# Latent stages of an RWKV-7 hybrid: TensorE's order written out, head products moved into the chain's gaps

## Chip, cores and metric

One core of one Trainium2 chip runs the whole kernel. The metric is the device time of one execution in microseconds (us); the median of several runs is compared. The profiler records one execution, every instruction on the five engines: TensorE (PE, with its weight loads as PEld), VectorE (DVE), ScalarE (ACT), GpSimd (POOL) and SyncE (SP), the last two used here mostly to issue DMAs.

## What is computed

Two layers over 512 latent tokens and 256 context tokens of width 1024. The first ("even") layer is where the change lies. Its time mixing has 16 heads of 64, and per head and direction (forward and backward) a state S of 64 x 64 that is carried over the tokens:

```python
def step(S, inp):
    r_t, w_t, k_t, v_t, kk_t, a_t = inp
    sa = jnp.einsum("bhvk,bhk->bhv", S, -kk_t)
    S = (S * w_t[:, :, None, :]
         + sa[..., None] * (kk_t * a_t)[:, :, None, :]
         + v_t[..., None] * k_t[:, :, None, :])
    return S, jnp.einsum("bhvk,bhk->bhv", S, r_t)
```

The context tokens run first, and their final states start the scan over the latent tokens. The decay w and the factor a come from low-rank products (tanh and sigmoid of two thin matrices). In parallel runs a gated short convolution: four projections per 128 channels (cg, xb, bg, zb), a product, a three-tap filter and gates. An output projection joins both. The second ("odd") layer is a gated convolution module, which the change does not touch.

## The kernel before

The scan is done in chunks of 64 tokens, so the 512 latent tokens are 8 chunks (NLAT) and a chain has 8 steps. Heads are handled in pairs. There are twelve stages, `for s in range(12)` (L898): stages 0 to 3 run the context chains (two head pairs each), stages 4 to 11 the chains of latent pairs 0 to 7. While the chain of stage s runs, the same stage prepares later pairs. `STAGE` (L35) holds the order in which this is written for latent stages, "OSPLHFC":

- O, `po`: the bonus term of pair s+1, one product.
- S, `solve` (L629): the triangular inverse of each chunk of pair s+1. VectorE transposes Nt to X (L637), then does 31 pairs of dependent instructions, a product (L643) and an addition (L645); this text calls them the sweep. Two transposes follow (L648, here R1, and L649, R2). Then ScalarE copies R1 into E (L654), TensorE does the first merge (64 matmul records, 32 x 32), ScalarE copies Gs, TensorE does the second merge, ScalarE copies the result into E.
- P and L, `prep_lat` (L390) and `light` (`light0` L422, `lightz` L493): loads k, v, r of pair s+2 and makes its low-rank factors, normalised kk, and the operands AR and BK, one half for each direction z.
- H, `heavy` (L568): the head products of pair s+2. "A" makes four groups of 8 matmuls, A.B per chunk, which VectorE masks into E (L588); "N" copies diagonal blocks into Nt (L605, four copies on ScalarE); "B" transposes BK into BKt; "V" makes the centred v into UV.
- F, `finish` (L780): normalises the output O of pair s, transposes it and applies gate and bonus.
- C, `conv_branch` (L810): the dense projections of one 128-channel group of the convolution, 4 x 8 x 3 matmuls of 128 x 512. Three per product, since hi and lo parts are kept apart: `mm3` multiplies hi by hi, hi by lo and lo by hi. A weight half tile is loaded by DMA, cast to its hi part on ScalarE (L125), and subtracted to its lo part on VectorE (L126).

`chain_lat` (L723) is one chain step. It has three places where TensorE waits for another engine: after the products into zo, ScalarE copies Zs (L743); after the products into uh, ScalarE makes two UV copies (L749); after the products with BKt, VectorE updates H (L756, two instructions).

The order on each engine comes from a planner that simulates the program and takes, of the instructions that are ready on an engine, the one that was written first. What is written earlier thus goes first on ScalarE and VectorE too. Two means bend this: `pinned()` (L548) ties each matmul of a group to the one before, so that they keep the written order among themselves; the whole chain uses one such object, `cmm`. And `issue_after` puts a block behind a given instruction: `LIGHT_AFTER`, `HEAVY_AFTER` and `CONV_AFTER` name the chain steps behind which low-rank, head and dense products may start. Between those, the planner alone mixes dense and head products into the chain's gaps.

PSUM has eight banks of 128 x 512: two under the tag "at" (head and low-rank products), one each under mm0 and mm1 (projections), two under zo (chain), and uh0 and uh1. Weight half tiles have two buffers for the raw load and three each for hi and lo. Operands AR have six buffers, BK two, E and UV two each.

Of the kernel before, what the change touches and what calls it, by code (L numbers as in the profile page):

```python
# [8 lines left out]
F32 = mybir.dt.float32  # L9
# [20 lines left out]
LIGHT_AFTER = ((0, None, 0), (None, 1, 4))  # L30
HEAVY_AFTER = ((3, None, 3, 2), (5, None, None, None))
CONV_AFTER = (0, 2, 7, 6)
PA_ORDER = ((0, 1), (1, 0), (1, 1), (0, 0))
HEAVY = ("VBOAN", "ANBV")
STAGE = ("OFPLSH", "OSPLHFC")  # L35
# [16 lines left out]
def kernel(ctx: ExitStack, tc: tile.TileContext, I: dict, out: bass.AP):  # L52
# [6 lines left out]
    def mm3(o, ah, al, bh, bl, start, stop):  # L59
        T.matmul(o, ah, bh, start=start, stop=False)  # L60
        T.matmul(o, ah, bl, start=False, stop=False)  # L61
        T.matmul(o, al, bh, start=False, stop=stop)  # L62
# [52 lines left out]
    env = {"lo": V}  # L115
# [13 lines left out]
    def outproj(m0, tags, ks, held, early=lambda k: (None, None, None)):  # L129
        acc = [[bank(f"o{m0 + m}{n}", tags[2 * m + n]) for n in range(2)] for m in range(2)]  # L130
        for k in ks:
            y, yr, ws = early(k)
            if y is None:
                y = op.tile([P, 512], F32R, tag="y", name=f"y{m0}_{k}", bufs=4)
            yh, yl = y[:, 0:256], y[:, 256:512]
            if (m0, k) == (0, 7):
                hilo(oT7[:, 0:256], None, yh, yl, None)
            else:
                if yr is None:
                    yr = op.tile([P, 256], F32, tag="yr", name=f"yr{m0}_{k}", bufs=4)  # L140
                hilo(ysp[k, :, m0 * P : m0 * P + 2 * P], yr, yh, yl)
            if k not in held:
                if ws is None:
                    ws = [op.tile([P, D], F32, tag="wr", name=f"wr{m0}_{k}", bufs=3)] + [
                        op.tile([P, D], F32R, tag="w", name=f"w{x}{m0}_{k}", bufs=6) for x in "hl"]
                held[k] = hilo(wo[k * P : (k + 1) * P, :], *ws)
# [243 lines left out]
    def prep_lat(p):  # L390
        st = state(True, p)
        st["H"] = w("h0", f"h0_{p}")[:, 0:P].rearrange("p (z x) -> p z x", z=2)
        for which in (1, 2, 0):
            t = w("rkv"[which] + "_", "rkv"[which] + st["nm"])
            nc.gpsimd.dma_start(t, psp[p, which])
            st["rkv"[which]] = t
        nc.gpsimd.dma_start(st["H"], h0d[p].rearrange("p (z x) -> p z x", z=2))
        return st

# [14 lines left out]
    def light(st, an=None):  # L414
        la = LIGHT_AFTER[an is not None and an["lat"]]
# [6 lines left out]
    def light0(st):  # L422
# [23 lines left out]
        def low_(i, z, name):  # L446
            pl = ps_at(name)
            if lat:
                rows = slice(64 * i, 64 * i + 64)
                mm(pl, lwh[:, i, z, :], lorl[i][z], True, False)  # L450
                mm(pl, lwl[rows, z, :], lorl[i][z][rows], False, True)
# [10 lines left out]
        mm(pl, blk, sq, True, True)  # L462
# [105 lines left out]
    def heavy(st, an=None):  # L568
        ha = (None,) * 4 if an is None else HEAVY_AFTER[an["lat"]]
        lat, nm = st["lat"], st["nm"]  # L570
        v_ = st["v"]
# [4 lines left out]
        def pa():  # L576
            for gi, (z, g) in enumerate(PA_ORDER if lat else ((0, 0), (1, 0))):
                with anchored(an, ha[gi if lat else 2 * gi]):
                    AR, BK = st["AR"][z], st["BK"][z]
                    m, x = (4, P) if lat else (8, CH)  # L580
                    c0 = m * g
                    pas = [ch3(ps_at(f"pa{nm}{z}{g}{h}"), x) for h in range(2)]
                    go = pinned()
                    for c in range(m):
                        for h in (1, 0):
                            go(pas[h][:, c, :], kb(BK, h, c0 + c), AR[ZR[h], c0 + c, 0:x])
                    for h in range(2):
                        V.tensor_tensor(out=E[:, h, z * NLAT + c0 : z * NLAT + c0 + m, :], in0=pas[h],  # L588
                                        in1=maskE[:, z * (1 + h) : z * (1 + h) + 1, 0:x].to_broadcast([P, m, x]), op=ALU.mult)

        def pb():
            for z in range(2):
                pbs = [ch3(ps_at(f"pb{nm}{z}{h}")) for h in range(2)]
                go = pinned()
                for c in range(NLAT):
                    for h in (1, 0):
                        go(pbs[h][:, c, :], kb(st["BK"][z], h, c), ident[ZR[h], ZR[h]], op=tr)
                for h in range(2):
                    S.copy(st["BKt"][z][:, :, ZR[h]], pbs[h])
# [7 lines left out]
        def pv():  # L607
            pv = ch3(ps_at(f"pv{nm}"))
            for c in range(NLAT):
                for h in range(2):  # L610
                    mm(pv[ZR[h], c, :], v_[ZR[h], c * CH : (c + 1) * CH], ctr[ZR[h], ZR[h]], True, True)
# [6 lines left out]
        def po():  # L618
            if lat:
                bon = st["bon"]  # L620
                pb = ps_at("pbon" + nm)
                mm(pb, blk, bon, True, True)
                V.scalar_tensor_tensor(out=bon, in0=pb, scalar=0.5, in1=v_, op0=ALU.mult, op1=ALU.mult)

        st["po"] = po
        for x in HEAVY[lat]:
            {"A": pa, "B": pb, "N": nt, "V": pv, "O": po}[x]()

    def solve(st):  # L629
        nm, E = st["nm"], st["E"]  # L630
        Xt = w("X", "X" + nm)
# [18 lines left out]
        Gs = Xt[:, 0:512].rearrange("p (a b) -> p a b", b=32)  # L650
# [4 lines left out]
        pg = px = uhs[1]  # L655
        top = [slice(64 * z, 64 * z + 32) for z in range(2)]
        low = [slice(64 * z + 32, 64 * z + 64) for z in range(2)]
        for q in range(16):
            for z in range(2):
                mm(pg[low[z], q * 32 : q * 32 + 32], E[top[z], 1 - z, q, 32:64], R2[top[z], q, :],  # L660
                   True, True)
        for z in range(2):
            S.copy(Gs[low[z]], ch3(pg[low[z]], 32))
        for q in range(16):
            for z in range(2):
                mm(px[top[z], q * 32 : q * 32 + 32], Gs[low[z], q, :], R1[low[z], q, :], True, True)
# [56 lines left out]
    def chain_lat(st, i):  # L723
# [19 lines left out]
        S.copy(Zs, zo[:, 0:2, :])  # L743
        for h, z in hz:
# [3 lines left out]
        for h in range(2):  # L748
            u_ = S.copy(UV[ZR[1 - h], i : 2 * nch - i : 2 * nch - 1 - 2 * i, ZR[h]], uh[ZR[1 - h], 0:2, :])  # L749
        h_ = None  # L750
# [16 lines left out]
        else:  # L767
            o = O[:, nch - 1 - i : i + 1 : 2 * i + 1 - nch, :]
            V.tensor_tensor(out=o, in0=zo[:, 2:4, :], in1=o, op=ALU.add)

    def gate(p, cb, nm):
# [3 lines left out]
        g = cvp.tile([P, SEQ], F32, tag="gz", name=f"g{nm}{p}")  # L775
        S.activation(g, pz, AF.Tanh, scale=0.5)
        V.scalar_tensor_tensor(out=g, in0=g, scalar=1.0, in1=pz, op0=ALU.add, op1=ALU.mult)
        return g

    def finish(st):  # L780
# [10 lines left out]
        go = pinned()  # L791
# [15 lines left out]
    def after(anchor):  # L807
        return tc.issue_after(anchor) if anchor is not None else nullcontext()

    def conv_branch(p, an=None):  # L810
        anchors = [None if an is None or x is None else an[x] for x in ((0, 2, 4, 6) if p == 7 else CONV_AFTER)]
        with after(anchors[0]):
            wt = load_w(40 + p, f"cg{p}")
            pcg = ps_mm(f"pcg{p}")
            proj(wt, pcg, hlat)
        cg = cvp.tile([P, SEQ], F32, tag="cg", name=f"cg{p}")
        S.copy(cg, pcg)
        with after(anchors[1]):
            wt = load_w(48 + p, f"xb{p}")
            pxb = ps_mm(f"pxb{p}")  # L820
            proj(wt, pxb, hlat)
        V.tensor_tensor(out=cx[:, :, 1:65], in0=ch3(pxb), in1=ch3(cg), op=ALU.mult)
        yb = cvp.tile([P, SEQ], F32, tag="yb", name=f"yb{p}")
# [448 lines left out]
```

## Time and profile before

| what | us |
|---|---|
| median of 3 runs | 1514.84 (1505.89 to 1517.57) |
| profiled execution, its own time | 1506.4 |
| its span (first to last instruction) | 1504.6 |
| PE busy, DVE busy, ACT busy | 1429.3, 964.3, 766.4 |
| latent chains, first Zs copy to last stage's end | 541.5 to 1004 |
| second layer, after 1105 | 399 |

A row of a timeline reads: start, duration, engine, line of the kernel, operation, output<-inputs, shape, count; in brackets the idle time of that engine before it and what ended it. A row of a table of groups reads: line, engine, operation, tiles, shape, count | busy us, mean ns of one | idle us before, and what ended it. A row of a table by window reads: window, its length, then for each engine busy us and the number of instructions, the granted TensorE clock (1 is full), the share of time in which the DMA engines were busy, GB/s. An fp32 matmul leaves two records, so a group of 4 shows as x8. Tile names ending in l belong to latent pairs, in c to context pairs. Helpers hide the caller's line: L57 is every fp32 matmul, L60 to L62 the three dense ones of `mm3`.

### The profile page before, as it was taken

How to read it: one execution, taken by the hardware profiler on the slowest of the kernel's cores; microseconds unless marked ns; L12 is line 12 of the kernel's file. 1: busy time of each engine (PE TensorE's matmuls, PEld its weight loads, DVE VectorE, ACT ScalarE, POOL GpSimd, SP SyncE). 2: the span in 40 equal slices, each digit the busy share in tenths (PEclk: the TensorE clock that was granted, in tenths of full speed). 3: DMA queues.
4: the chain of work that ended last, by engine and by line, in shares of the span. 5: the costliest groups of instructions: out<-in, count | busy, mean ns of one | idle time of the engine just before them, and what ended most of it. 6: DMA issues, size and time to landing. Idle time of an engine off the chain costs nothing.

```text
span 1504.6 us, 29614 instructions
## 1 busy us (share of the span) xinstructions
PE 1429.3 (95%) x11857; PEld 1014.2 (67%) x11857; DVE 964.3 (64%) x2242; ACT 766.4 (51%) x1552; POOL 152.3 (10%) x263
## 2 busy tenths in 40 slices
PE   5699999999998999999999999999999999999998
PEld 1374577878776766666666666677757666688876
DVE  2575587558696978888788887658544525434333
ACT  4323465364755575755757657546553414363322
POOL 0533210000110101011011000001100000000000
PEclk9899999979997999999999999999999999999999
DMA  8644533212232312231222212468403303033222
GB/s 316 174 130 164 162 113 99 89 57 67 80 89 77 89 60 74 67 91 51 80 72 68 79 46 82 152 221 293 159 20 112 103 10 113 28 112 99 94 88 84
DMA packets 136650, 156.59 MB, mean 104 GB/s; under 512 B 15266, under 2 KB 104034, under 8 KB 136512
## 3 DMA queue, kind: packets, MB, share of 16 engines
q1 hardware_dynamic: 119952, 104.37, 22.4%
q0 software_dynamic: 15488, 49.14, 10.1%
q8 instruction: 93, 1.52, 0.4%
q10 hardware_dynamic: 1072, 1.19, 0.2%
q14 instruction: 45, 0.37, 0.1%
HBM read 137.36 MB, written 17.31 MB: 103 GB/s over the span
## 4 chain that ended last, share of the span: by engine, by line
PE 46%; ACT 6%; DVE 5%; DMA 2%; issue 2%; DVEq 0%; SPq 0%; ACTq 0%
PE pu L61 4%; PE pu L62 4%; PE pu L60 4%; PE zol L57 3%; PE uh L57 2%; PE f L61 2%; PE f L60 2%; PE f L62 2%; PE pz L61 2%; PE pz L62 2%; PE pz L60 2%; PE px L57 2%; PE pc L57 1%; PE pal L57 1%; PE o L62 1%
## 5 line engine op out<-in xcount | busy, mean ns | idle before, releaser
L57 PE MATMUL pal<-ARl,BKl 64*128 64x128 f32 x512 | 59.1, 311 | 6.3 <-DVE xtmpc L643 4.3
L645 DVE TENSOR_TENSOR Yl<-Yl,xtmpl 128x126 f32<-128x126 f32 (+22 forms) x248 | 62.5, 252 | 2.2
L643 DVE TENSOR_TENSOR xtmpl<-Xl,Yl 128x126 f32<-128x126 f32 (+22 forms) x248 | 62.4, 252 | 2.0
L57 PEld LDWEIGHTS pal<-ARl,BKl 64*128 64x128 f32 x512 | 44.2, 199 | 25.8 <-DVE E L588 6.2
L57 PE MATMUL zol<-UV,E 64*64 64x64 f32 (+1 forms) x1024 | 54.2, 221 | 0.0
L61 PE MATMUL o<-wl,y 128*128 128x512 f32 x124 | 50.0, 403 | 4.3 <-DVE wl L126 4.3
L57 PE MATMUL zol<-Hl,ARl 64*64 64x64 f32 x896 | 50.2, 230 | 2.3 <-DVE Hl L756 2.3
L1091 DVE TENSOR_TENSOR a<-pu,a 128x512 f32<-128x512 f32 x16 | 11.1, 692 | 62.0 <-PE pu L62 59.7
L749 ACT COPY UV<-uh 64x128 f32<-64x128 f32 x128 | 33.4, 261 | 33.2 <-PE uh L57 30.9
L126 DVE TENSOR_TENSOR wl<-wr,wh 128x1024 fp32r<-128x1024 f32 x28 | 37.1, 1323 | 20.7 <-ACT wh L125 20.5
L588 DVE TENSOR_TENSOR E<-pal,maskE 128x512 f32<-128x512 f32 x64 | 43.5, 685 | 10.4 <-PE pal L57 10.2
L60 PE MATMUL o<-wh,y 128*128 128x512 f32 x124 | 49.6, 401 | 0.5 <-ACT wh L125 0.5
L62 PE MATMUL o<-wh,y 128*128 128x512 f32 x124 | 49.9, 403 | 0.0
L57 PEld LDWEIGHTS zol<-Hl,ARl 64*64 64x64 f32 x896 | 35.0, 133 | 21.2 <-issue 16.9
L1096 ACT CAST ah<-a 64x512 fp32r<-64x512 f32 x32 | 19.8, 620 | 56.3 <-DVE a L1091 55.9
L756 DVE SCALAR_TENSOR_TENSOR Hl<-uh,PCl,HPl 128x64 f32<-128x64 f32 x112 | 26.8, 282 | 30.4 <-PE uh L57 21.4
L57 PEld LDWEIGHTS uh<-UV,BKt 128*64 128x64 f32 x704 | 26.8, 138 | 27.5 <-ACT UV L749 21.5
L57 PEld LDWEIGHTS zol<-UV,E 64*64 64x64 f32 (+1 forms) x1024 | 42.5, 136 | 2.8 <-ACT UV L749 2.1
L125 ACT CAST whcg<-wrcg 128x512 fp32r<-128x512 f32 x16 | 9.9, 621 | 63.5 <-DMA wrcg<-in_ev_w_in_dram 51.2
L57 PE MATMUL uh<-UV,BKt 128*64 128x64 f32 x704 | 36.9, 234 | 3.6 <-ACT UV L749 2.8
L125 ACT CAST wh<-wr 128x1024 fp32r<-128x1024 f32 x28 | 29.4, 1051 | 21.4 <-PE o L61 11.9
L57 PEld LDWEIGHTS uh<-Ol,E 64*64 64x64 f32 x512 | 19.9, 133 | 25.8 <-ACT Ol L743 17.4
(972 smaller groups left out, 4434.6 us busy)
## 6 DMA issues: line engine op xcount, KB each, us to landing
wr<-in_ev_w_out_dram SPq DMA_DIRECT2D x28, 512.0 KB, 5.0
mwr<-in_mod_w_dram POOLq DMA_DIRECT2D x32, 256.0 KB, 4.2
mwo<-in_mod_w_dram POOLq DMA_DIRECT2D x32, 256.0 KB, 3.2
ectx<-in_mod_w_dram SPq DMA_DIRECT2D x12, 512.0 KB, 5.1
wrk<-in_ev_w_in_dram SPq DMA_DIRECT2D x16, 256.0 KB, 2.9
wrv<-in_ev_w_in_dram SPq DMA_DIRECT2D x16, 256.0 KB, 2.9
wrr<-in_ev_w_in_dram SPq DMA_DIRECT2D x16, 256.0 KB, 2.9
wrza<-in_ev_w_in_dram SPq DMA_DIRECT2D x16, 256.0 KB, 2.8
```

What stands on the lines that cost most here:

```text
L57: return T.matmul(o, lhsT, rhs, start=start, stop=stop)
L60: T.matmul(o, ah, bh, start=start, stop=False)
L61: T.matmul(o, ah, bl, start=False, stop=False)
L62: T.matmul(o, al, bh, start=False, stop=stop)
L125: S.copy(hi, raw)
L126: env["lo"].tensor_tensor(out=lo, in0=raw, in1=hi, op=ALU.subtract)
L588: V.tensor_tensor(out=E[:, h, z * NLAT + c0 : z * NLAT + c0 + m, :], in0=pas[h], in1=maskE[:, z * (1 + h) : z * (1 + h) + 1, 0:x].to_broad ...
L643: V.tensor_tensor(out=tv, in0=X[:, :i, i : i + 1].to_broadcast([P, i, m]), in1=Y[:, i : i + 1, c0:].to_broadcast([P, i, m]), op=ALU.mult)
L645: V.tensor_tensor(out=Y[:, :i, c0:], in0=Y[:, :i, c0:], in1=tv, op=ALU.add)
L749: u_ = S.copy(UV[ZR[1 - h], i : 2 * nch - i : 2 * nch - 1 - 2 * i, ZR[h]], uh[ZR[1 - h], 0:2, :])
L756: h_ = V.scalar_tensor_tensor(out=Hn[:, z, :], in0=uh[:, 2 + z, :], scalar=PC[z][:, i : i + 1], in1=HP[:, z, :], op0=ALU.mult, op1=ALU.add)
L1096: S.copy(ahl[s][hr], a[hr])
```

## The change

In stages 4 to 10 every matmul goes through the one pinned object `cmm`, so TensorE runs exactly in the order in which the program is written. `chain_lat` gets a `fill` argument and calls it at its three waits in each step; each call takes the next unit off a list.

The list of stage s holds, in this order: six half groups of head products of pair s+1 with one of its two transposes and the opening of pair s+2's low-rank part among them, the first low-rank half of pair s+2, the last two half groups, the second transpose, `ready` (Nt copies and half of V), `settle` (the other half of V and the sweep), the second low-rank half, the bonus product, and 32 dense units of three matmuls each. 24 units fall into the chain's 8 x 3 waits. The remaining 24 follow in a row, with `finish` ahead of the unit numbered 10 (`LEAD`, counted from 0), and the two merges ahead of the last 7 and the last 3 units (`MERGE`). In stage 10 no pair is two ahead, so the low-rank units are missing and dense units move up.

So the head products are made one stage before their chain and no longer two, in the same stage as their sweep. Stage 3 no longer makes any; stages 4 to 10 make one pair each, and stage 10 had none before. The groups are ordered by z, the second to fourth use banks mm0 and mm1. Weight half tiles are loaded two ahead, by the unit that starts on a half tile. v of a pair is loaded a stage later than k and r. Stage 11 and the context stages keep their form.

```diff
-    def chain_lat(st, i):
+    def chain_lat(st, i, fill=lambda: None):
...
         S.copy(Zs, zo[:, 0:2, :])
+        fill()
...
+        fill()
         h_ = None
...
+        fill()
...
+    halves = [(p, nm, cb, b) for p in range(1, 8) for nm, cb in CONV for b in range(2)]
+    loaded = {}
+
+    def load_next():
+        if halves:
+            p, nm, cb, b = halves.pop(0)
+            lo_for(nm)
+            src = w_in[:, (cb + p) * P : (cb + p + 1) * P].rearrange("(k p) c -> p k c", p=P)
+            loaded[p, nm, b] = w_half(src[:, 4 * b : 4 * b + 4, :], f"{nm}{p}{b}")
+
+    def conv_units(p):
+        d, accs = {}, {}
+
+        def unit(nm, kt):
+            if kt == 0:
+                accs[nm] = ps_mm(f"p{nm}{p}")
+            ks = slice(kt % 4 * P, kt % 4 * P + P)
+            wh, wl = loaded[p, nm, kt // 4]
+            mm3(accs[nm], wh[:, ks], wl[:, ks], hlat[0][:, kt, :], hlat[1][:, kt, :], kt == 0, kt == KT - 1)
+            if kt % 4 == 0:
+                load_next()
+            if kt == KT - 1:
+                conv_after(p, nm, accs[nm], d)
+
+        return [lambda nm=nm, kt=kt: unit(nm, kt) for nm, _ in CONV for kt in range(KT)]
...
+    def lat_stage(s, st):
+        if s == 11:
+            env["go"] = mm
+            for i in range(NLAT):
+                chain_lat(st, i)
+            finish(st)
+            return
+        env["go"] = cmm
+        nx, far = sts[s + 1], None
+        if "v" not in nx:
+            prep_load(nx, 2)
+        if s == 4:
+            load_next()
+            load_next()
+        u = heavy(nx)
+        sweep, ma, mb = solve_parts(nx)
+        if s < 10:
+            far = prep_lat(s - 2)
+            sts.append(far)
+        A, B = u["A"], u["B"]
+
+        def light_unit(x):
+            return [] if far is None else [lambda: light0(far) if x is None else lightz(far, x)]
+
+        def ready():
+            u["N"][0]()
+            u["V"][0]()
+
+        def settle():
+            u["V"][1]()
+            sweep()
+
+        units = (A[0:4] + B[0:1] + light_unit(None) + A[4:6] + light_unit(0) + A[6:8] + B[1:2] + [ready, settle]
+                 + light_unit(1) + u["O"] + conv_units(s - 3))
+        n = [0]
+
+        def fill():
+            if units:
+                units.pop(0)()
+
+        for i in range(NLAT):
+            chain_lat(st, i, fill)
+        at = {LEAD: lambda: finish(st), len(units) - MERGE[0]: ma, len(units) - MERGE[1]: mb}
+        for k, f in enumerate(units):
+            if k in at:
+                at[k]()
+            f()
...
-            elif x == "H" and s < 10:
+            elif x == "H" and s < 3:
                 heavy(sts[s + 2], st)
```

More of the change, by code (lines that the diff above doesn't have):

```diff
@@ L414, in light @@
     def light(st, an=None):
-        la = LIGHT_AFTER[an is not None and an["lat"]]
+        la = LIGHT_AFTER
         with anchored(an, la[0]):
@@ L649, in solve, with merge_a @@
         V.transpose(R2, R1)
-        Gs = Xt[:, 0:512].rearrange("p (a b) -> p a b", b=32)
+        d.update(R1=R1, R2=R2, Xt=Xt)
+    pg = px = uhs[1]
+    top = [slice(64 * z, 64 * z + 32) for z in range(2)]
+    low = [slice(64 * z + 32, 64 * z + 64) for z in range(2)]
+    def merge_a(st, E, d):
+        R1, R2, Xt = (d[k] for k in ("R1", "R2", "Xt"))
+        d["Gs"] = Gs = Xt[:, 0:512].rearrange("p (a b) -> p a b", b=32)
         for z in range(2):
@@ L774, in gate @@
         proj(wt, pz, hlat)
[L775 to L778, printed above, removed]
+        return gated(p, nm, pz)
     def finish(st):
```

241 lines of the change are left out of this document (135 added, 106 removed).

## The prediction

> **What bounds the kernel now.** I read the page first, then a table of busy time by stage, then the timeline of one stage on each engine.
>
> ```profile
> PE 1429.3 (95%) x11857; PEld 1014.2 (67%) x11857; DVE 964.3 (64%) x2242; ACT 766.4 (51%) x1552; POOL 152.3 (10%) x263
> ```
>
> TensorE is called 95% busy, but matmul records overlap, so that share cannot say what is left to gain. The stages of the latent pairs (s = 4 to 10), cut at the first Zs copy of each chain, say more:
>
> ```profile
> core 0: us, PE busy (x) PEld busy (x) DVE busy (x) ACT busy (x) POOL busy (x), PEclk, DMA share, GB/s
> 541.50:606.90 65.40, 62.64 (x825) 42.55 (x825) 51.31 (x158) 43.30 (x100) 6.73 (x12) 1.00 0.22 66
> 606.90:668.70 61.80, 58.75 (x772) 40.20 (x772) 51.70 (x148) 39.98 (x95) 6.75 (x12) 1.00 0.25 71
> ...
> 915.80:958.60 42.80, 42.02 (x623) 28.93 (x623) 32.64 (x111) 22.27 (x61) 2.16 (x4) 1.00 0.15 42
> ...
> 479.00:541.50 62.50, 62.00 (x626) 45.14 (x626) 55.86 (x146) 41.09 (x82) 6.91 (x13) 1.00 0.31 93
> ```
>
> Stage 4 takes 65.4 us, the five like stages 5 to 9 308.9 us together (606.9 to 915.8; 61.8 each), stage 10, which prepares no pair, 42.8. In each like stage two engines are nearly full: TensorE, and VectorE with 51.7 of 61.8 us. One chain step on TensorE (start, duration):
>
> ```profile
> 749.24 0.27 PE L57 MATMUL uh<-Ol,E 64*64 64x64 f32 x2
> ...
> 749.64 0.50 PE L60 MATMUL pxb<-hlh,whxb 128*128 128x512 f32 x1
> 749.98 0.40 PE L61 MATMUL pxb<-hll,whxb 128*128 128x512 f32 x1
> 750.32 0.45 PE L57 MATMUL uh<-UV,BKt 128*64 128x64 f32 x8
> 750.61 0.40 PE L57 MATMUL zol<-UV,E 128*64 128x64 f32 x8
> 750.94 0.50 PE L62 MATMUL pxb<-hlh,wlxb 128*128 128x512 f32 x1
> 751.27 0.40 PE L60 MATMUL pxb<-hlh,whxb 128*128 128x512 f32 x1
> 751.60 0.45 PE L57 MATMUL zol<-Hl,ARl 64*64 64x64 f32 x8
> 751.88 0.40 PE L57 MATMUL zol<-UV,E 64*64 64x64 f32 x8
> 752.21 0.71 PE L57 MATMUL pal<-ARl,BKl 64*128 64x128 f32 x6
> ```
>
> Start to start, the three parts of a step cost 0.40, 0.62 and 0.61 us: 1.63. Each of its gaps is filled by two dense products at 0.67 us. In a long row a dense product costs 0.23:
>
> ```profile
> 762.35 0.39 PE L61 MATMUL pbg<-hll,whbg 128*128 128x512 f32 x1
> 762.58 0.40 PE L62 MATMUL pbg<-hlh,wlbg 128*128 128x512 f32 x1
> ```
>
> So a change of form costs 0.67 - 0.46 = 0.2 us, and that is what long rows can save. The other engine has a loop of its own, seen where a stage ends:
>
> ```profile
> 780.91 1.11 DVE L648 STREAM_TRANSPOSE Nt<-Yl 128x512 f32<-128x512 f32 x1
> ...
> 782.05 2.51 ACT L654 COPY E<-Nt 32x512 f32<-32x512 f32 x4 [1.21 <-DVE Nt L648]
> ...
> 782.82 1.20 PE L57 MATMUL uh<-Yl,E 32*32 32x32 f32 x64 [0.22 <-DVE Yl L649]
> ...
> 790.68 2.13 DVE L637 STREAM_TRANSPOSE Xl<-Nt 128x1024 f32<-128x1024 f32 x1 [1.78 <-ACT Nt L605]
> ```
>
> The sweep of pair s+1 ends at 780.91 and its two merges follow (782.82 is the first). The next sweep, X at 790.68, starts only 9.8 us after the end of this one, because the products of pair s+2 were made a stage ahead. VectorE then fills a whole stage with that sweep and everything else by turns:
>
> ```profile
> 759.96 0.28 DVE L643 TENSOR_TENSOR xtmpl<-Xl,Yl 128x126 f32<-128x126 f32 x1
> 760.16 0.69 DVE L541 TENSOR_TENSOR ARl<-rl,Pl 128x512 f32<-128x512 f32 x1
> 760.76 0.28 DVE L645 TENSOR_TENSOR Yl<-Yl,xtmpl 128x126 f32<-128x126 f32 x1
> ```
>
> A dependent sweep step waits for the one before it, the planner puts any ready instruction into that hole, and a 0.69 us instruction delays the sweep by 0.60. The more VectorE work is ready, the longer a sweep lasts:
>
> ```profile
> 728.80:781.00 52.20, 47.50 (x149) 1.00 0.23 68
> 914.70:948.10 33.40, 28.19 (x97) 1.00 0.18 52
> ```
>
> These are two sweeps on VectorE from the transpose X to the transpose R1: 52.2 us in a like stage, 33.4 in stage 10, with the same 62 sweep steps. Now 52 us does no harm, since the sweep has a whole stage.
>
> **The change, part by part.** The arithmetic, the loads and nearly all instructions stay. Of each like stage the change moves:
>
> (a) Head products, masks and Nt of pair s+1 from stage s-1 into stage s, in front of the sweep of the same pair. This is the part that decides. The loop of one stage becomes: chain start, products, masks, Nt, sweep, merges, next chain start. I add it up from the chain's start.
>
> TensorE up to the last head product: eleven units (eight half groups, one transpose group, the sums of squares and one low-rank unit) and nearly four steps. Six records of a head group last 0.71 us (752.21), so a unit of eight, its change of form included, about 0.8, eight of them 6.4; transposes, sums of squares and the low-rank unit I take at 0.85, 0.9 and 1.7, estimates from the dense cost with its change of form; chain parts 3 x 1.63 + 0.61 + 0.40 = 5.9. Together 15.8. Two masks follow, then four Nt copies, priced by the four E copies of the same shape at 782.05: 2.5.
>
> ```profile
> L588 DVE TENSOR_TENSOR E<-pal,maskE 128x512 f32<-128x512 f32 x8 | 5.5, 686 | 0.5 <-PE pal L57 0.5
> ...
> L517 ACT ACTIVATE kdl<-al,oka,hka 128x512 f32<-128x512 f32 x2 | 1.6, 821 | 0.0
> ```
>
> Masks: 2 x 0.6 = 1.2. On top come waits that the trace of before lacks: the units are written between the chain steps, so ScalarE's eight instructions of a low-rank half (the row above is one of them, about 5.6 us in all) now stand ahead of the copies of later chain steps; before, the whole chain was written ahead of them. Bounds 0 (they run in ScalarE's idle time) and 5.6 (all in the way); I take 2, as ScalarE is idle a third of a like stage (39.98 of 61.8). X then starts at 15.8 + 1.2 + 2.5 + 2.0 = **21.5** us.
>
> Sweep: stage 10's 33.4 us is the nearest row, but seven chain steps lie in it and only about three do after; each step's H update holds VectorE for its own time and the wait before it:
>
> ```profile
> L756 DVE SCALAR_TENSOR_TENSOR Hl<-uh,PCl,HPl 128x64 f32<-128x64 f32 x14 | 3.4, 285 | 2.8 <-PE uh L57 2.5 <-ACT whbg L125 0.4
> ```
>
> (3.4 + 2.8) / 7 = 0.89 a step, four steps 3.5, which leaves 29.9. The low-rank unit written right behind the sweep adds nine VectorE instructions, 8 x 0.6 + 1.2 - 1.1 = 4.9 (the last term is the hole they fill, 0.12 each). **34.8**; bounds 29.9 (they run after the sweep) and 40.
>
> Tail, written in TensorE's order: R1 1.1, E copies 2.5, merge 1.2 and two changes of form 0.4, four dense units 4 x 0.69, merge 1.2 and 0.4, three units 2.1: **11.6**, with the Gs copies hidden under the four units.
>
> The stage is then 21.5 + 34.8 + 11.6 = 67.9 us instead of 61.8. Five stages 339.5 - 308.9 = +30.6; stage 4, 67.9 - 65.4 = +2.5.
>
> (b) Stage 10 now carries a pair's head products. Without low-rank units its last head product is nine fills in: 3 x 1.63 + 6.4 + 0.85 = 12.1, with masks, Nt and a wait of 1.0 X starts at 16.8; sweep 29.9, tail 11.6: 58.3 against 42.8, **+15.5**.
>
> (c) Stage 3 loses one pair's head work.
>
> ```profile
> L57 PE MATMUL pal<-ARl,BKl 64*128 64x128 f32 x64 | 6.6, 291 | 0.0
> ```
>
> TensorE and VectorE are both full there (62.0 and 55.86 of 62.5), masks alone are 5.5 us of VectorE: **-6**, bounds -8 and -3.
>
> (d) Long dense rows. In a like stage TensorE needs 8 x 1.63 = 13.0 for the chain; fills of 6.4 + 1.7 + 0.9 + 3.4 + 1.2 (V) + 0.9 (O) + 8 x 0.9 (dense) = 21.7; behind the chain 24 x 0.69 = 16.6, merges 2.4, finish 1.2, changes of form 1.0. That is 55.9, some 6 us less than now. It is worth nothing while the loop of (a) is longer: TensorE waits 12 us a stage instead.
>
> (e) v is loaded a stage later and half tiles are loaded two ahead; a half tile serves four units, 2.8 us or more, and two lie ahead: zero, covered by those units. Were the cover gone, one ScalarE cast and one VectorE subtraction, 1.3 us a half tile, would show.
>
> Sum: +30.6 + 2.5 + 15.5 - 6 = +42.6 on the profiled execution's own 1506.4 us: 1549. The three runs have a median of 1514.84, 8.4 above it; I set half of that: **1553 us**.
>
> **Rivals.** *TensorE sets the stage.* If VectorE gets the sweep done under the long row, a stage is 55.9 and a bit: 56.5. Five stages -26.4, stage 4 -8.9, stage 10, with no low-rank work and three more dense units among its fills, 13.0 + 20.1 + 19.1 = 52.2 (+9.4), stage 3 -6: -32, or 1474 to 1483 us. For it speaks that of VectorE's work only the H updates and the dense halves' subtractions have to lie inside the sweep; against it the alternation at 759.96 and the 33.4 us of stage 10.
>
> *The loop comes out as long as now.* With no waits on ScalarE (19.5), the second low-rank half after the sweep (29.9) and the same tail, a stage is 61.0: -3.9 over five stages, stage 4 -4.4, stage 10 15.8 + 29.9 + 11.6 = 57.3 (+14.5), stage 3 -6: 0, 1507 to 1515 us.
>
> *The clock falls in TensorE's new waits,* 12 us a stage. Once in this trace it waited 4.29 us:
>
> ```profile
> 452.00:456.50 4.50, 0.23 (x2) 0.01 (x1) 4.50 (x10) 0.61 (x1) 1.03 (x2) 0.80 0.43 135
> 456.50:475.00 18.50, 17.24 (x200) 13.62 (x200) 8.26 (x15) 6.41 (x12) 0.54 (x1) 0.50 0.23 67
> ```
>
> Afterwards the granted clock was 0.50 for 18.5 us. One such spell a stage, a fifth of it on the path, costs 0.5 x 3.7 = 1.8 us in seven stages: +13, 1566; with half on the path 1585. In the like stages of before the clock is 1.00.
>
> [...]
>
> **Chances.** The longer loop at full clock 0.46, the same with the clock falling 0.10, TensorE setting the stage 0.25, loop as long as now 0.19. Faster by over 1% 0.25, within 1% 0.19, slower by over 1% 0.56; 1% is about what a measurement of this kernel can tell, its three runs being 0.8% apart. The range 1478 to 1585 takes in most of the faster case and the worse clock case; the likeliest case alone is 1530 to 1575 (waits 0 to 5.6, sweep 32 to 38).
>
> **What would show it.** Right: in the profile after, X of a like stage starts about 21 us behind the chain's start, R1 some 35 us later, the stage is 66 to 70 us and stage 10 is 56 to 60; TensorE's longest waits stand before the merge and in the chain behind ScalarE or VectorE; dense products run at 0.23. Wrong: R1 before the long row is through, merges without a wait, stages of 57 us; or a sweep that runs bare of other VectorE work.

## The result, and the profile after

The changed kernel takes 1578.95 us (median of 4 runs, 1576.71 to 1583.88) against 1510.37 (4 runs, 1504.58 to 1517.57) for the kernel before beside it: ratio 1.0469, 95% interval 1.0422 to 1.0516. It is slower by 4.7%. The profiled execution took 1583.88 us, with a span of 1582.1; it is the slowest of its four, so the profiled spans lie 77.5 us apart and the medians 68.6. Its page, engine totals, shows the same 11857 matmul records and more time for them:

```profile
PE 1440.6 (91%) x11857; PEld 1044.2 (66%) x11857; DVE 981.4 (62%) x2242; ACT 769.5 (49%) x1552; POOL 151.3 (10%) x263
```

The table by stage (stages 3, 4, 5, 6 and 10), cut at the first Zs copy of each latent chain; the first row starts at 479.0 in both kernels, which is a time inside stage 3 and not a Zs copy:

```profile
479.00:524.30 45.30, 45.30 (x390) 33.18 (x391) 42.20 (x116) 31.23 (x66) 5.84 (x11) 0.98 0.30 88
524.30:613.50 89.20, 71.21 (x930) 54.03 (x932) 63.33 (x177) 48.70 (x108) 7.28 (x13) 0.85 0.23 66
613.50:684.80 71.30, 59.45 (x776) 44.10 (x774) 54.32 (x154) 40.40 (x94) 6.74 (x12) 0.88 0.21 61
684.80:757.30 72.50, 61.40 (x776) 44.60 (x776) 54.35 (x154) 40.58 (x94) 6.74 (x12) 0.84 0.21 60
...
972.40:1033.60 61.20, 54.93 (x767) 40.99 (x764) 39.27 (x121) 29.12 (x74) 2.15 (x4) 0.94 0.13 42
```

The third number from the right is the granted clock: 1.00 in every latent stage before, 0.84 to 0.88 in the like stages now. Against the prediction's terms (profiled spans, 1582.1 - 1504.6 = 77.5):

| part | predicted | measured |
|---|---|---|
| like stages 5 to 9 | +30.6 | 358.9 - 308.9 = +50.0 |
| stages 3 and 4 | -6 + 2.5 | 134.5 - 127.9 = +6.6 |
| stage 10 | +15.5 | 61.2 - 42.8 = +18.4 |
| all else | 0 | +2.5 |

Where does a like stage lose its time? TensorE's waits in stage 5, by what it waited for (us in total, times, longest), are all in the chain or in a fill between its steps:

```profile
PE zol L57 <- DVE Hl L810: 6.5, 3, 4.6
PE uh L57 <- ACT Ol L795: 3.0, 2, 2.2
PE uh L57 <- ACT UV L802: 1.4, 2, 0.9
PE lal L57 <- ACT UV L614: 0.7, 1, 0.7
```

That is 11.6 us, and no merge is among them. The longest wait, 4.6 us, seen on VectorE: the H update of chain step 5 (L810; steps are counted from 0) comes at 652.15. Ahead of it, from 644.47 on, VectorE alternates between steps of the sweep and the nine instructions of the second low-rank half:

```profile
644.47 1.25 DVE L511 TENSOR_TENSOR_SCAN Pl<-scm,sg 128x528 f32<-128x528 f32 x1
...
650.54 0.69 DVE L545 SCALAR_TENSOR_TENSOR BKl<-al,iPl 128x512 f32<-128x512 f32 x1
651.15 0.28 DVE L687 TENSOR_TENSOR xtmpl<-Xl,Yl 128x126 f32<-128x126 f32 x1
651.35 0.68 DVE L546 TENSOR_TENSOR BKl<-kdl,iPl 128x512 f32<-128x512 f32 x1
651.95 0.28 DVE L689 TENSOR_TENSOR Yl<-Yl,xtmpl 128x126 f32<-128x126 f32 x1
652.15 0.28 DVE L810 SCALAR_TENSOR_TENSOR Hl<-uh,PCl,HPl 128x64 f32<-128x64 f32 x1
```

The wait of 2.2 us is the same thing on ScalarE: the copy of Zs of chain step 3 (L795) stands behind the last instructions of the first low-rank half:

```profile
628.83 0.72 ACT L529 ACTIVATE bonl<-kdl,cols 128x512 f32<-128x512 f32 x1
629.46 0.63 ACT L514 ACTIVATE Pl<-Pl 128x528 f32<-128x528 f32 x1
630.11 0.61 ACT L547 COPY BKl<-BKl 64x512 f32<-64x512 f32 x1
630.75 0.20 ACT L516 COPY PCl<-Pl 128x8 f32<-128x8 f32 x1
630.86 0.26 ACT L795 COPY Ol<-zol 128x128 f32<-128x128 f32 x1
```

The sweep of the same stage, X and R1 on VectorE, the last E copy on ScalarE, and TensorE at the first merge:

```profile
638.23 2.09 DVE L681 STREAM_TRANSPOSE Xl<-Nt 128x1024 f32<-128x1024 f32 x1 [3.48 <-ACT Nt L601]
...
668.20 1.18 DVE L692 STREAM_TRANSPOSE Nt<-Yl 128x512 f32<-128x512 f32 x1
...
672.59 0.62 ACT L706 COPY E<-Nt 32x512 f32<-32x512 f32 x1
...
676.02 0.39 PE L57 MATMUL pzb<-hlh,wlzb 128*128 128x512 f32 x1
676.34 1.20 PE L57 MATMUL uh<-Yl,E 32*32 32x32 f32 x64
```

The E copies end at 673.2, the merge follows its predecessor in the long row at 676.34: what it needs had been there for 3 us. Last, the granted clock over this stage, cut where it changes:

```profile
613.50:627.40 13.90, 11.93 (x211) 8.56 (x208) 10.76 (x30) 7.71 (x23) 1.07 (x2) 1.00 0.14 44
627.40:637.60 10.20, 7.83 (x119) 6.65 (x118) 6.07 (x11) 7.78 (x21) 0.00 (x0) 0.50 0.01 2
637.60:651.30 13.70, 7.76 (x106) 4.53 (x98) 12.62 (x34) 8.56 (x19) 1.64 (x4) 1.00 0.13 40
651.30:658.10 6.80, 5.24 (x46) 3.50 (x47) 5.94 (x22) 2.61 (x7) 2.88 (x5) 0.50 0.36 116
658.10:684.80 26.70, 26.70 (x320) 20.86 (x320) 18.93 (x59) 13.74 (x26) 1.15 (x2) 1.00 0.32 90
```

Half clock for 17.0 us in two spells: the first follows the wait of 1.38 us that ends at 626.97, the second begins inside the one of 4.6 us, which ends at 652.86. The row behind the chain (last line) has no wait and full clock.

### The profile page after: what moved, and what is told of

Its sections match the earlier page's. It is cut to its first block, busy times and chain, and to the rows that moved or that the text cites. A ratio compares the mean times of both kernels' runs of the same rounds, so it can differ in the third digit from the quotient of the medians.

```text
span 1582.1 us, 29611 instructions
## 1 busy us (share of the span) xinstructions
PE 1440.6 (91%) x11857; PEld 1044.2 (66%) x11857; DVE 981.4 (62%) x2242; ACT 769.5 (49%) x1552; POOL 151.3 (10%) x263
## 5 line engine op out<-in xcount | busy, mean ns | idle before, releaser
L57 PE MATMUL zol<-Hl,ARl 64*64 64x64 f32 x896 | 57.6, 255 | 37.4 <-DVE Hl L810 37.4
L57 PE MATMUL o<-wh,y 128*128 128x512 f32 x248 | 79.5, 397 | 0.6 <-ACT wh L126 0.5
L57 PEld LDWEIGHTS zol<-Hl,ARl 64*64 64x64 f32 x896 | 41.1, 155 | 56.6 <-DVE Hl L810 33.7
L689 DVE TENSOR_TENSOR Yl<-Yl,xtmpl 128x126 f32<-128x126 f32 (+22 forms) x248 | 62.6, 252 | 4.4
L687 DVE TENSOR_TENSOR xtmpl<-Xl,Yl 128x126 f32<-128x126 f32 (+22 forms) x248 | 62.6, 253 | 3.9
L57 PE MATMUL zol<-UV,E 64*64 64x64 f32 (+1 forms) x1024 | 58.3, 239 | 0.0
L57 PEld LDWEIGHTS o<-wh,y 128*128 128x128 f32 x248 | 45.8, 188 | 10.6 <-ACT wh L126 1.2
L57 PE MATMUL uh<-Ol,E 64*64 64x64 f32 x512 | 32.5, 254 | 19.1 <-ACT Ol L795 17.8
L57 PEld LDWEIGHTS zol<-UV,E 64*64 64x64 f32 (+1 forms) x1024 | 47.0, 153 | 2.9 <-ACT UV L802 2.8
L126 ACT CAST wh<-wr 128x1024 fp32r<-128x1024 f32 x28 | 29.4, 1049 | 22.5 <-PE o L57 11.6
L810 DVE SCALAR_TENSOR_TENSOR Hl<-uh,PCl,HPl 128x64 f32<-128x64 f32 x112 | 28.1, 277 | 15.8 <-ACT UV L802 9.2
L57 PE MATMUL pcg<-hlh,whcg 128*128 128x512 f32 x64 | 35.9, 561 | 0.0
L772 ACT ACTIVATE HPl<-Hl,PCl 128x64 f32<-128x64 f32 x96 | 28.1, 339 | 11.4 <-DVE Hl L810 10.7
L687 DVE TENSOR_TENSOR xtmpc<-Xc,Yc 128x126 f32<-128x126 f32 (+22 forms) x124 | 31.5, 254 | 2.9
```

The costliest lines, as they stand in the source:

```text
L57: return T.matmul(o, lhsT, rhs, start=start, stop=stop)
L126: S.copy(hi, raw)
L687: V.tensor_tensor(out=tv, in0=X[:, :i, i : i + 1].to_broadcast([P, i, m]), in1=Y[:, i : i + 1, c0:].to_broadcast([P, i, m]), op=ALU.mult)
L689: V.tensor_tensor(out=Y[:, :i, c0:], in0=Y[:, :i, c0:], in1=tv, op=ALU.add)
L772: S.activation(t[:, z, :], H[:, z, :], AF.Copy, scale=st["PC"][z][:, i : i + 1])
L810: h_ = V.scalar_tensor_tensor(out=Hn[:, z, :], in0=uh[:, 2 + z, :], scalar=PC[z][:, i : i + 1], in1=HP[:, z, :], op0=ALU.mult, op1=ALU.add)
```

## The experiments

Theory A, formed from these rows: the planner gives ScalarE and VectorE whatever is ready and written first. Before, the whole chain was written ahead of the stage's other work; now head masks, low-rank halves and the sweep are written between the chain's steps, so they stand ahead of the later steps' copies and H updates. TensorE, tied to one order, waits. Rival B is the prediction's own: the loop through the sweep ends the stage. Theory C: the half clock costs by itself. Each run is compared with runs of the kernel before on the same chip; stage times are those of the profiled execution, like stages as a mean of stages 5 to 9. In the last three rows and in "finish first, led" units stand ahead of the first latent chain, so part of stage 4 is counted to stage 3.

| kernel | median us | ratio to before (95%) | stage 4 | like stage | stage 10 |
|---|---|---|---|---|---|
| before | 1510 | 1 | 65.4 | 61.8 | 42.8 |
| changed | 1579.0 | 1.0469 (1.0422-1.0516) | 89.2 | 71.8 | 61.2 |
| chain first | 1569.6 | 1.0395 (1.0342-1.0448) | 89.2 | 71.4 | 56.5 |
| low-rank half late | 1615.4 | 1.0690 (1.0634-1.0745) | 97.8 | 78.2 | 59.1 |
| half sweep | 1580.0 | 1.0454 (1.0384-1.0524) | 89.6 | 71.7 | 56.2 |
| waits filled | 1562.9 | 1.0330 (1.0269-1.0391) | 89.4 | 69.4 | 59.3 |
| chain and finish first | 1592.8 | 1.0552 (1.0511-1.0593) | 91.9 | 74.1 | 58.8 |
| unpinned | 1529.2 | 1.0131 (1.0087-1.0175) | 71.0 | 64.0 | 58.7 |
| chain and finish first, half sweep | 1521.6 | 1.0076 (1.0039-1.0112) | 84.0 | 63.6 | 53.2 |
| unpinned, chain first | 1518.5 | 1.0026 (0.9993-1.0059) | 76.6 | 62.6 | 62.2 |
| finish first, led | 1602.0 | 1.0608 (1.0579-1.0636) | 66.0 | 75.5 | 59.2 |
| heads early | 1590.2 | 1.0509 (1.0475-1.0543) | 68.4 | 74.3 | 54.8 |
| spread | 1506.9 | 0.9980 (0.9955-1.0006) | 60.1 | 59.1 | 55.9 |
| spread, ends mended | 1517.5 | 1.0055 (1.0020-1.0090) | 77.6 | 59.3 | 52.4 |

**Chain first.**

```
+        with tc.high_priority():
+            S.copy(Zs, zo[:, 0:2, :])
```

(the planner takes what stands under `high_priority` ahead of all else that is ready) and the same around the UV copies, the H update, HP and the output copy or add.

> The changed kernel with one thing more: the chain's own ScalarE and VectorE instructions (copy of Zs, copies of UV, H update, HP scaling, output copy or add) are put ahead of everything else that is ready on their engines; TensorE's written order stays. Theory A (TensorE waits inside the chain, because the head products, low-rank halves and sweep instructions that are now written between the chain's steps stand ahead of the chain's copies and H updates on ScalarE and VectorE): the waits of 1.4, 2.2 and 4.6 us ahead of products of the chain in a like stage shrink to under 1 us each, the half-clock spells of 17 to 24 us a stage go with them, a like stage falls from 71.3-72.5 us to 57-64, and the kernel from 1579 to 1490-1535. Rival B (the prediction's: the sweep ends the stage): the sweep is only cut up more, a like stage stays at 68-72, the kernel at 1565-1590.

The waits of theory A went as it said, and the stage stayed: 71.4 instead of 71.8. Stage 5's waits are now others:

```profile
PE po L57 <- DVE Ol L853: 5.8, 1, 5.8
PE lal L57 <- ACT UV L614: 2.6, 1, 2.6
PE pvl L57 <- ACT BKt L595: 2.1, 1, 2.1
```

`po`, the finish's product, stands in the long row, and its VectorE instructions stood behind the sweep's. The other two wait for a bank ("at") that a ScalarE copy, now later, has still to empty. The numbers are those of rival B (68 to 72 us, 1565 to 1590), but not by its mechanism: no merge is among the waits. A had left out what comes next.

**Low-rank half late.**

```
-                 + light_unit(1) + u["O"] + conv_units(s - 3))
+                 + u["O"] + cv[0:8] + light_unit(1) + cv[8:])
```

> The changed kernel with one unit moved: the second half of the low-rank work of the pair after next is written behind the chain (after the first eight units of the dense products) instead of in its sixth step. Theory A: the 4.6 us wait ahead of the sixth step's H update and the half-clock spell behind it (6.8 us) go, 4 to 8 us of each of six stages, if the sweep keeps its place: 1530-1555. Rival B (sweep ends the stage): the sweep has nine instructions fewer in its way but the stage's tail has them more: 1570-1585.

A miss for both. The 4.6 us wait is gone, and the long row waits 13.8 us for the finish, whose VectorE work now stands behind sweep and low-rank half:

```profile
678.55 0.76 PE L57 MATMUL po<-ident,Ol 64*64 64x64 f32 x9 [13.76 <-DVE Ol L847]
```

**Half sweep.**

```
-        for i in range(31, 0, -1):
+        for i in range(15 if st['lat'] and st['p'] else 31, 0, -1):
```

> The changed kernel, leaving out part of the computation: for pairs 1 to 7 of the latent stages the sweep runs only its last 15 of 31 iterations (half of its VectorE work, about 14 us of the 30 us from X to R1). Rival B (sweep ends the stage): a like stage is 8 to 14 us shorter, the kernel 1480-1525. Theory A (waits in the chain set the stage; TensorE does not wait at the merges): only the sweep instructions that stand ahead of the chain's H updates matter, 0 to 4 us a stage: 1550-1579.

Half of VectorE's sweep left out is worth nothing: 71.7 us a like stage, and 1580.0 us is 1 us above what theory A expected. The sweep does not end the stage. B falls, for the changed kernel as it is.

**Waits filled.** Ahead of the chain's products that wait 1.4, 2.2 and 4.6 us, TensorE gets products whose result is overwritten (the cut shows two of the three places):

```
+        junk({3: 3, 6: 12}.get(i, 0) if env["go"] is not mm and p < 6 else 0)
         for h, z in hz[::-1]:
             m0_ = cmm(zo[ZR[1 - h], z, :], ...
```

> The changed kernel with idle work for TensorE in three waits of each of six latent stages: 3, 5 and 12 products of 128x128 by 512 columns (0.32 us each at full clock, into a bank that nothing reads before it is overwritten) ahead of the chain's products that wait 1.4, 2.2 and 4.6 us. Nothing else waits less. Theory C (the half-clock spells that follow these waits cost by themselves): the spells of 17 to 24 us a stage at half clock go, a like stage is 4 to 9 us shorter, the kernel 1525-1555. If the clock costs nothing because the chain waits anyway: 1575-1590.

16 us faster by the medians, with more work: the clock costs by itself, 2.4 us a like stage here. That is less than theory C expected (4 to 9 us a stage, 1525 to 1555). It is a lower bound, since the clock is still 0.93 in stage 5 (0.98 in stage 6) and some waits were not filled.

**Chain and finish first.** The finish's square, reduction, inverse root and scaling get the same `high_priority`.

> The kernel with the chain's ScalarE and VectorE instructions first, and in addition those of the pair's finish (square, reduction, inverse root, scaling of the output) put ahead of the sweep. In the run with the chain first alone, the waits inside the chain were down to 2.1 and 2.6 us, and a new one of 5.8 us stood in the long row, at the finish's product, which the written order puts ten units behind the chain while its VectorE instructions stood behind the sweep's. Theory A2 (the written order ties TensorE to whichever work of ScalarE and VectorE is last in their queues, so a wait only moves until both are taken first): the 5.8 us go, a like stage falls from 71 to 63-67, the kernel to 1525-1550. Rival B (the sweep ends the stage): the sweep ends later by the finish's 4 us, the merges wait for it, a like stage stays at 69-72, the kernel at 1560-1580.

Slower again, outside both expectations, and the wait is where rival B wanted it. Stage 6:

```profile
PE uh L57 <- DVE Yl L693: 7.9, 1, 7.9
PE lal L57 <- ACT UV L614: 2.4, 1, 2.4
PE pvl L57 <- ACT BKt L595: 2.1, 1, 2.1
```

`uh<-Yl` is the first merge, waiting for R2. What is put ahead of the sweep makes the sweep end later: in stage 5 it takes 39.1 us from X to R1, against 30.0, while the chain, from its first to its last Zs copy, takes 38.5 us, against 46.7. The sweep lost 9 us where the chain won 8. From this came theory D: two limits stand side by side, the waits in the chain, and VectorE's queue from the masks through the sweep to the merge; lifting one shows the other.

**Chain and finish first, half sweep.** Both edits in one kernel.

> The kernel with chain and finish first, and the half sweep too (it leaves out 16 of the 31 iterations for pairs 1 to 7 of the latent stages, about 14 us of VectorE a stage). Halving the sweep alone had moved nothing (1580), and taking chain and finish first had moved the last wait to the merge that needs the sweep (7.9 us). Theory D (two limits stand side by side at 71 us a like stage: the waits in the chain, and VectorE's queue from the head masks through the sweep to the merge; each hides the other): with both lifted a like stage falls to 61-66 us and the kernel to 1510-1545. If the sweep's end is only the place where something else shows (ScalarE's copies, banks, the clock): 70-75 us a stage, 1575-1600.

63.6 us a like stage, clock 0.89 in stage 5, and what is left are the two bank waits:

```profile
PE pvl L57 <- ACT BKt L595: 2.1, 1, 2.1
PE lal L57 <- ACT UV L614: 2.1, 1, 2.1
```

The four kernels make a square: 1579 as changed, 1580 with half the sweep, 1593 with chain and finish first, 1522 with both. Alone worth -1 and -14, together +57. Both expectations of theory D came (61 to 66 us, 1510 to 1545), and the 7.9 us at the merge are gone from the waits. Theory D is shown by that.

**Unpinned.** Only the chain's products keep their written order; units stay where they are written, and the planner chooses.

```
-        env["go"] = cmm
+        env["lat"] = True
```

(with `mm` for `cmm` in the head units)

> The changed kernel without the one written order: only the products of the chain keep theirs, and each bank's dense or head products are free to go whenever they are ready, in the planner's order; units and the order in which they are written stay. If the written order itself costs the time (TensorE could have gone ahead while the chain waited): a like stage 62-66, the first latent stage 70-78, the kernel 1515-1550. If the planner's order on ScalarE and VectorE costs it, whatever TensorE may do: like stages 69-72, the kernel 1560-1585.

50 us come back by this alone. The written order itself is thus what turns these delays into time: the planner lets TensorE take a dense product while a chain product waits. In the stage after 600.7 it waits for nothing longer than 0.8 us and the clock is full:

```profile
600.70:660.00 59.30, 57.88 (x770) 41.04 (x769) 51.59 (x156) 39.53 (x94) 6.73 (x12) 1.00 0.26 74
```

One of its five like stages took 75.5 us, the others 59.1 to 62.6. In that one TensorE waited 2.0 us for R2 ahead of a merge, from 724.0 on, and then ran at half clock for 30.7 us:

```profile
725.80:756.50 30.70, 30.02 (x396) 23.53 (x399) 15.81 (x38) 17.82 (x44) 1.50 (x3) 0.50 0.10 31
```

Half of that, 15 us, is about what the stage is longer than the mean of the others (61). It is the plainest price of the clock in these traces, though from one execution.

**Unpinned, chain first.**

> The kernel without the one written order (1529 us), with the chain's ScalarE and VectorE instructions first as well. If its remaining loss comes from chain steps of 17 to 20 us, in which the H update stands behind head masks and low-rank instructions on VectorE, the chain shortens and the kernel gets 1490-1520. By theory D (VectorE's queue up to the merge is the other limit) the head masks and with them the sweep only come later, and the kernel stays at 1520-1560.

1518.5, inside the first expectation by 1.5 us and as far from the second: like stages 62.6 instead of 64.0, stage 4 5.6 us longer. It tells little.

**Finish first, led.** Nine units ahead of the first latent chain, and V's products to another bank (`ps_mm` for `ps_at`).

```
+        for _ in range(9 if s == 4 else 0):
+            fill()
```

> The kernel with chain and finish first, and two things more: in the first latent stage nine units are written ahead of the chain, whose second step waits for the sweep before it; and the products of V with the centring matrix go to another bank, since they and the low-rank products behind them waited 2.1 and 2.6 us for copies out of the two banks that they share. Expected by theory A2: the first latent stage falls from 89 to 70-76 us, the two waits and the half-clock spells behind them go (4 to 6 us of each of six stages), a like stage is near TensorE's own 56 us (57-61), the kernel 1470-1505. If the bank waits only move to the next copy: like stages 63-66, 1510-1535.

A miss. Stage 4 fell to 66.0 only because the nine units count to stage 3 now: from the last product of the context chains to the end of stage 4 it takes 116.9 us, against 116.4 with chain and finish first. The like stages rose to 75.5. The bank waits became one of 4.0 us at V, for which the profile names no releaser, and one of 1.0, and the merge waits 7.9 us as before. That nothing else can show while the sweep is the limit is argued here; the two edits were not run apart.

**Heads early.** As in the kernel before, head products are made a stage ahead, but in the written order: those of pair s+2 between the merges at the end of stage s, in "at" banks. The chain's gaps get dense units.

```
+            units[k:] = [ma] + F[0:2] + units[k : k + 1] + F[2:4] + units[k + 1 : k + 2] + [mb] + F[4:6] + units[k + 2 :] + F[6:8]
```

> The kernel with chain and finish first, one written order for TensorE, and the head products moved: those of the pair after next, which need neither chain nor merges, are written between the merges at the end of the stage instead of in the next chain's gaps (with nine units ahead of the first latent chain). The chain's gaps take dense products in their place, and the sweep can start some 15 us earlier after the chain's start. By theory D both limits fall together: a like stage 58-63 us, the first latent stage 64-70, the kernel 1470-1515. If TensorE's written order costs through any other queue (banks, ScalarE), a like stage stays at 66-72 and the kernel at 1540-1580.

A miss: 74.3. In stage 5 X now starts 3.5 us behind the chain's first Zs copy, but low-rank units and transposes stood one behind the other in the first two steps, which took 11.6 and 12.6 us. The longest waits of stage 6:

```profile
PE po L57 <- DVE Ol L854: 2.4, 1, 2.4
PE lwl L57 <- ACT BKt L595: 2.2, 1, 2.2
PE pb1l L566 <- ACT al L507: 1.4, 1, 1.4
```

**Spread.** The same, with the units of a stage written so that dense units (c) stand between those that depend on each other (l, z0, z1 low-rank, B transposes, N Nt copies and half of V, V its other half and the sweep, F head products of pair s+2):

```
+MIX = {4: ..., 5: "l c c B0 N c V c c z0 c c B1 c c O z1", 10: ...}
+TAIL = ("F0 F1 c c c c c c c F2 F3 c c c c F4 F5 fin c c ma c mb F6 F7", ...)
```

> As the kernel with the heads early (chain and finish first, one written order, head products of the pair after next written at the end of a stage), but spread: the low-rank units, transposes and products of V, which stood one behind the other in the first two chain steps and made those 12 us each, have dense products between them, the finish stands just ahead of the merges, and the head products stand between long rows of dense products. Theory D with the written order's corollary (a unit of TensorE waits in the row unless what it needs was begun a unit's length per instruction earlier): no wait of TensorE over 1.5 us is left, with them go the half-clock spells, a like stage is 57-62 us, the kernel 1465-1500, faster than both. If VectorE's queue (some 55 us busy a stage) cannot be filled so densely, the wait shows at the first merge and a like stage is 63-67, the kernel 1510-1545.

The stage came as expected, the kernel did not. Stage 5, table by window and the longest waits:

```profile
600.20:659.00 58.80, 55.00 (x774) 38.80 (x772) 52.69 (x153) 40.47 (x93) 6.75 (x12) 1.00 0.25 74
```

```profile
PE uh L60 <- ACT UV L807: 1.2, 2, 0.8
PE lal L60 <- ACT sg L504: 0.8, 1, 0.8
PE zol L60 <- DVE Hl L816: 0.7, 2, 0.6
```

All waits together are 4.0 us, none over 0.8, the clock is full. Yet 1506.9 us cannot be told from the kernel before (0.998, 0.9955 to 1.0006). The five like stages won 308.9 - 295.4 = 13.5 us; stage 10 gave back 13.1:

```profile
895.60:951.50 55.90, 49.92 (x704) 35.70 (x704) 35.22 (x110) 28.43 (x72) 1.60 (x3) 0.97 0.14 42
```

It has 704 matmul records, where the kernel before had 623: work that stood a stage earlier there. The profiled spans still differ by 6.9 us (1497.7 and 1504.6), but this execution is the fastest of its ten and is 8.4 us ahead already in the context chains of stage 2, which the edit does not touch.

**Spread, ends mended.**

```
-        "fin c c c c c c ma c c c c mb c c c")
+        "c c c c c c c fin c ma c c c c mb c c c")
```

and dense units ahead of and between the head products of stage 4.

> The spread kernel with its two ends mended: in the first latent stage dense products stand ahead of and between the head products (which waited 2.6 us for a bank and made a dense product wait 2.1 us for masks), and in the stage of the last pair but one the finish stands seven dense products later (its product waited 3.6 us) and the products of V one later (1.2 us). Expected: the first latent stage with the stage before it 3 to 7 us shorter, the stage of the last pair but one 4 to 6 us shorter, the kernel 1494-1501, ratio to the kernel before 0.989-0.995. If TensorE's work is the bound already and the waits only move: 1503-1510. Either way no more than some 20 us under the kernel before can be had by order alone, since TensorE is busy 1429 of 1505 us there and 1408 of 1498 us in the spread kernel.

1517.5 us misses both expectations. Stage 10 won 3.5 us, stage 4 lost 17.5 (in both kernels its chain starts at 540.1): the dense units taken to the front were missing behind the chain, where TensorE now waited for the merge and for the masks:

```profile
PE uh L60 <- DVE Yl L696: 3.4, 1, 3.4
PE pzb L60 <- DVE cx L882: 2.5, 1, 2.5
PE pa01l L60 <- DVE E L590: 2.3, 2, 2.0
```

No version beat the kernel before.

## Why the prediction was right and wrong

**Slower, and the size.** Right in sign; 1579 lies in the range, 4 us above the likeliest case's own 1530 to 1575 and inside the band of the falling clock (1566 to 1585). The number is in part luck: +42.6 us was the sum of a loop that does not end the stage, and what did cost the time stood in it with 2 us.

**(a) The loop through the sweep ends the stage.** This step failed. The prediction named what would show it wrong: "R1 before the long row is through, merges without a wait, stages of 57 us". The first two are what the trace shows, the third is not: 25.8 us from the chain's first product to X (predicted 21.5), 30.0 for the sweep (34.8), and then a row that never waits, in a stage of 71.3 us. Halving the sweep moved nothing. The term that failed is "waits that the trace of before lacks", taken as 2 us with bounds 0 and 5.6, up to X: there TensorE waits 4.2 us, and 7.4 more behind X, for which the prediction had no term; together 11.6. It saw the cause, ScalarE's low-rank half ahead of later copies, but counted it only up to X and only on ScalarE. The worst wait is for VectorE, behind X, at the H update of step 5: the same low-rank half and the sweep itself stand ahead of the chain there. The loop was not far: its last E copy ends 3 us ahead of the merge, and with chain and finish first the loop sets the stage, at 74.1. A stage of 71.3 us is TensorE's work of 54.8 (58.8 less 4.0 of waits, spread kernel), 11.6 us of waits, and 4.9 left over, for which 13.1 us of work at half clock is the only candidate that the rows show (a merge took 1.92 us at half clock, at 535.31, and 1.20 at full, at 676.34).

**The clock.** The prediction kept 0.46 for full clock and 0.10 for a fall. It fell in every stage from 4 to 10. The price it gave, 1.8 us a stage, rested on a fifth of a spell lying on the path; it is below the 2.4 us that filling the waits took off, itself a lower bound, and below the 4.9 left over. The chance was too low, though the prediction itself reckoned with 12 us of waits a stage. The one spell it went by came with a wait of 4.29 us; in the changed kernel one came with a wait of 1.38 us in every like stage (below).

**(b) Stage 10:** 61.2 measured, 58.3 predicted; its working, a loop through the sweep, fails as in (a): no merge is among TensorE's waits there, of which the longest, 2.4 us, is at the finish's product. Half the sweep took off 5.0 us and chain first 4.7; how these work there stays open. **(c) Stages 3 and 4** have to be taken together, as the cut between them has moved: the chain's first product of stage 4 now goes at 523.57, ahead of stage 3's last dense row and of the merges that the chain's next products need. Together they are 6.6 us longer, where -3.5 was predicted; 2.7 of these stand ahead of both, since the same products of stage 3's context chain go at 478.95 before and at 481.63 after. TensorE's waits from 524.3 to 547, at a granted clock of 0.77, stand around those merges:

```profile
PE pa00l L57 <- ACT gvr L1066: 2.9, 1, 2.9
PE uh L57 <- DVE Yl L693: 1.3, 1, 1.3
PE uh L57 <- ACT Xl L712: 1.3, 1, 1.3
PE uh L57 <- ACT E L720: 1.3, 1, 1.3
```

After 547 eleven more us of waits follow in stage 4, as in a like stage. The prediction took stage 4 for a like stage and did not ask what may go ahead of its chain in the written order.

**(d) Long rows:** dense products ran at 0.23 us and TensorE's need came out at 54.8 us (55.9 predicted): right, and worth nothing as long as the waits stand. **(e) Loads:** no wait for them is among those of stage 5, which are all shown; zero holds.

**Rival "TensorE sets the stage":** its 56.5 us are reached almost (59.1) when every wait is under 1 us, but not by this change, and the kernel does not gain: order alone moves work between stages.

## What to carry to other kernels

Fixing the order of one engine is only half an order: list for each of its instructions what the other engines must have done, and where that stands in their queues, or every delay there becomes a wait of all that follows. Where the stage does not move when a suspected limit is taken away, another of the same length may stand beside it: take both away in one kernel before dropping either. And what a new order wins in the repeated stages is to be counted again at the first and last of them, where the same work has less to hide behind.

## What the runs showed of the hardware

Apart from the last one of an execution (4.0 and 4.4 us), half clock came in spells of 3.4 to 20.5 us in the kernel before and of 3.4 to 23.9 us in the changed kernel, all multiples of 3.41 us, and in each of these two traces their starts lie whole multiples of 3.41 us apart; the row of 30.7 us in the unpinned kernel is 9 x 3.41. In the same two traces, from 100 to 1450 us, TensorE has nine waits of 2.38 us or more that begin at full clock (2.38 to 4.57 us). In each case a spell began within the wait or at most 1.95 us behind it. Of shorter waits only some had one: in the changed kernel a wait of 1.38 us in every like stage did, one of 2.14 us (from 1138.79) did not; a wait of 1.20 us at 225.6, the same in both kernels, had one of 20.5 us behind it in the changed kernel and none in the kernel before. In the kernel before a spell of 20.5 us (from 321.6) came with no wait over 0.9 us in the 90 us ahead of it. The window rows above show several spells; this is one more, behind the finish's wait of 3.6 us in stage 10 of the spread kernel:

```profile
937.90:941.30 3.40, 3.40 (x10) 2.63 (x9) 1.63 (x3) 0.62 (x1) 0.54 (x1) 0.50 0.20 77
```

What decides whether a short wait brings a spell, no run here shows.
